# Fetching the indexer's cached keys: 128 pages a gather, through DRAM, in place of 128 small gathers

## The chip, the cores and the metric

One core of a Trainium2 chip runs the whole kernel. Its engines work side by side, each through its own list of instructions in order: TensorE (PE) multiplies matrices, VectorE (DVE) and ScalarE (ACT) do elementwise work, GpSimd (POOL) does elementwise work and issues indirect DMAs, SyncE (SP) issues the other DMAs. The metric is the device time of one launch in microseconds. One launch was also taken by the hardware profiler; its records are the profile and the trace.

## The reference

The kernel computes one layer of a hybrid decoder for a prompt of 1024 tokens and a sample group of 8 sequences with 8 new tokens each (1088 tokens, model width 1024). The layer has a sparse attention branch and a gated linear attention branch (GLA), a gated merge, an output projection and an MLP. The sparse branch selects 256 keys for each query by a small indexer:

```python
def indexer_scores(q_idx, w_idx, k_idx):
    dots = jnp.einsum('bqhd,bsd->bqhs', q_idx, k_idx) * (IDX_DIM ** -0.5)
    return jnp.einsum('bqhs,bqh->bqs', jax.nn.relu(dots), w)   # w: scaled w_idx

# sample group: 4096 past keys of each sequence lie in pages of 128 keys
k_idx_past = cache_kidx[page_table].reshape(b, past, IDX_DIM)
k_idx_all = jnp.concatenate([k_idx_past, k_idx], axis=1)
```

`cache_kidx` has 320 pages of 128 keys by 64 dimensions in float32; `page_table` names 32 pages for each of the 8 sequences, so 256 pages of 32 KB, 8 MB in all, are fetched through an index. The prompt's scores use no cache. All sums are kept to float32 quality: each operand is split into a high part, rounded to the format that TensorE multiplies at full rate, and a low part (value minus high part), and three products are added.

## The kernel before, in words

All of the first phase is written by one function, `front`. Its pieces are Python generators ("streams"): `main` runs the projections in the order of the list `jobs` (a small `misc` block with the indexer keys, four blocks `qi` of indexer queries, `ka`, `va`, four `qa`, then for each of four heads `qb`, `kb` and the GLA values `psv`, then gates); `idx_prompt` makes the prompt's scores (`psi`); `idx_sample` makes the sample group's scores; `top_prompt` searches on DVE for the prompt's selection thresholds; `heads` is the GLA; others follow later. A planner (`Order.run`, `Clock`) keeps an estimate of when each engine and each tile would be ready and steps the first stream that could go on; what it writes down is a fixed order for each engine. Every operation is issued by one helper (L219 in the profile), so groups are told apart by the tiles' names.

A projection block is loaded by SP (`wr`, 512 KB), rounded by ACT (`wh`), and its low part `wl` = `wr` - `wh` is made by GpSimd or DVE: the function `sub` chooses by the planner's clocks, with a handicap for DVE as last argument. PE then runs groups of three matmuls, for instance `qa<-xh,wh`, `qa<-xl,wh`, `qa<-xh,wl`.

`idx_sample` goes through the past keys in 16 chunks of 16 pages. `i_load(n)` fetches a chunk into a page `kir` of 128 partitions (two pages by 64 dimensions) by 1024: eight indirect DMAs on GpSimd, each with 128 rows of 512 bytes; 128 in all. Three chunks are kept ahead. `split(n)` rounds the chunk on ACT (`kih`) and subtracts on DVE (`kil`, a new page). PE makes the products for each half chunk: three matmuls `pss`; ACT takes the rectified high part `rh`, DVE the low part `rl`, and three matmuls `po` sum over heads. Two chunks are fetched at the start and a third when the stream begins; the scores themselves wait for the end of `idx_prompt`.

`top_prompt` searches 32 bits. One round counts six times over score tiles (`jk<-sc`, the long instructions) and has six small steps on 128x3 numbers between them (`ga_m`, `ga_u`, `ga_f`, `gb_m`, `gb_u`, `gb_f`). It begins when `idx_prompt` ends and shares DVE with everything else. In the GLA's first head DVE prepares `gk`, for which PE's first `psas` waits.

In the second phase, `back`, there are 64 more gathers, `cvr<-vv`, of 128 rows of 2 KB for the attention values.

Of the kernel before, what the change touches and what calls it, by code (L numbers as in the profile page):

```python
# [12 lines left out]
F32 = mybir.dt.float32  # L13
F32R = mybir.dt.float32r
# [9 lines left out]
P = 128  # L24
# [23 lines left out]
NSM = 6  # L48
NSH = 6
KAHEAD = 2  # L50
VAHEAD = 1
SCRATCH = 4096
OBLEAD = 3
# [21 lines left out]
def f32(ap):  # L75
    return ap.bitcast(F32)


def view(ap, offset, dims):
    return bass.AP(tensor=ap.tensor, offset=ap.offset + offset, ap=[list(d) for d in dims])  # L80
# [254 lines left out]
def front(ph, tc, env, A, O):  # L335
# [13 lines left out]
    def page(name, dt=F32, shape=None):  # L349
        return clock.take(pgs.tile(shape or [P, T], dt, name=name, tag="pg", bufs=NPG), name, "pg", NPG)  # L350
# [9 lines left out]
    def cst(name, shape, dt=F32):  # L360
        return cs[0].tile(shape, dt, name=name, tag=name, bufs=1)
# [20 lines left out]

    ptab = page("ptab", I32, [P, 8, 32])
    sp.dma_start(ptab, view(A["page_table"], 0, [[0, P], [32, 8], [1, 32]]))
    jobs = []
    wt = {}

# [62 lines left out]
    p_q, p_b, p_64, p_32, p_n = (pf[:, i:i + 1] for i in range(5))  # L450


    ix_i = cst("ix_i", [P, 4, 32], I32)
    pm64 = cst("pm64", [P, 1])
    dve.tensor_scalar(pm64, p_n, -64.0, None, op0=OP.add)
    dve.tensor_scalar(ix_i[0:64], ptab[0:64, 0::2, :], 64.0, p_n[0:64], op0=OP.mult, op1=OP.add)
    dve.tensor_scalar(ix_i[64:128], ptab[64:128, 1::2, :], 64.0, pm64[64:128], op0=OP.mult, op1=OP.add)
    ix_k = const("ix_k", [1, 256], I32)
    dve.tensor_scalar(ix_k, ptab[0:1].rearrange("p a b -> p (a b)"), 128.0, None, op0=OP.mult)


    raw = {}
    i_order = [(qq, p) for qq in range(4) for p in range(4)]

    def i_load(n):
        qq, p = i_order[n]
        l = page(f"kir{qq}{p}", F32, [P, 1024])
        for g in range(8):
            pg = qq * 8 + g
            pool.indirect_dma_start(out=l[:, g * P:(g + 1) * P], out_offset=None, in_=A["ciT"],  # L470
                                    in_offset=bass.IndirectOffsetOnAxis(ap=ix_i[:, p, pg:pg + 1], axis=0))
        raw[n] = l


    for c, (c0, n) in enumerate(CH):
# [38 lines left out]
    brow = csg("brow", [64, 8])  # L514
    dve.tensor_scalar(brow, cb5[:64, :8], p_b[:64], None, op0=OP.is_equal)

    i_load(0)
    i_load(1)


    bcol = csg("bcol", [P, 8, 64], BF)
# [118 lines left out]
    def idx_prompt():  # L640
        yield lambda: s_wtok.done
        for grp in ((7,), (6,), (5,), (4, 2)):
            pg = page(f"sc{grp[0]}")
            o = 0
            for qt in grp:
                scp[qt] = pg[:, o:o + (qt + 1) * P]
                o += (qt + 1) * P
        scp[3] = small("sc3")
        dve.memset(f32(qz), 0.0)
        for h in range(8):  # L650
            yield lambda: h in qis
            q = qis.pop(h)
            yield [q[:, TP:T]]
            for e in range(2):
                r = ((h + e) % 2) * 64
                for b2 in range(2):
                    o = b2 * 64
                    src = q[r:r + 64, TP:T].rearrange("p (b q) -> p b q", q=8)[:, b2::2, :]
                    dve.tensor_copy(qz[o:o + 64, :, e, o + 8 * h:o + 8 * h + 8], f32(src))
            for qt in range(2, 8):  # L660
                w = (qt + 1) * P
                for k0 in range(0, w, 512):
                    n = min(512, w - k0)
                    lq = q[:, qt * P:(qt + 1) * P]
                    yield [lq]
                    ps = bank("psi")
                    pe.matmul(ps[:, :n], lq, kkh[:, k0:k0 + n], start=True, stop=False)
                    pe.matmul(ps[:, :n], lq, kkl[:, k0:k0 + n], start=False, stop=True)
                    r = small("r")
                    act.activation(r[:, :n], ps[:, :n], AF.Relu, scale=0.125)  # L670
                    sc = scp[qt][:, k0:k0 + n]
                    wc = wtok[:, qt, h:h + 1]
                    if h == 0:
                        dve.tensor_scalar(sc, r[:, :n], wc, None, op0=OP.mult)
                    else:
                        dve.scalar_tensor_tensor(sc, r[:, :n], wc, sc, op0=OP.mult, op1=OP.add)
                if h == 7:
                    d = scp[qt][:, qt * P:w]
                    pool.affine_select(d, d, pattern=[[-1, P]], compare_op=OP.is_ge, fill=NEG, base=0, channel_multiplier=1)
# [3 lines left out]
    ss = [page("ssa", F32, [P, TP]), page("ssb")]  # L683

    def idx_sample():
        i_load(2)
        dve.memset(ss[1][0:64, TP:T], NEG)

        def split(n):
            r = raw[n]  # L690
            h = page(f"kih{n}", F32R, [P, 1024])
            l = page(f"kil{n}", F32R, [P, 1024])
            act.activation(h, r, AF.Copy)
            dve.tensor_sub(l, r, f32(h))
            raw[n] = (h, l)
        yield [raw[0]]
        split(0)
        yield lambda: s_wtok.done
        cq = iota_f("cq", [4, 8, 8], [[0, 4], [0, 8], [1, 8]])
        cb = iota_f("cb", [4, 8, 8], [[-2, 4], [1, 8], [0, 8]])  # L700
# [8 lines left out]
        wsel = cst("wsel", [P, 512], F32R).rearrange("p (e a b) -> p e a b", e=2, b=64)  # L709
        act.activation(wsel[:, 0], wsf, AF.Copy)  # L710
        dve.tensor_sub(wsel[:, 1], wsf, f32(wsel[:, 0]))
        yield lambda: s_ip.done

        def chunk(p, kh, kl, n):
# [16 lines left out]
        for qq in range(4):  # L731
            po = [bank("po0", True), bank("po1", True)]
            pend = None
            for p in range(4):
                n = qq * 4 + p
                if n + 3 < 16:
                    i_load(n + 3)
                if n + 1 < 16:
                    yield [raw[n + 1]]
                    split(n + 1)  # L740
                kh, kl = raw.pop(n)
                for e in range(2):
                    s = slice(e * 512, e * 512 + 512)
                    yield [kh[:, s], kl[:, s], qz]
                    r = chunk(p, kh[:, s], kl[:, s], 512)
                    if pend:
                        yield [pend[1][1]]
                        sums(*pend)
                    pend = (p, r, 512, po[e], p == 0, p == 3)
            yield [pend[1][1]]  # L750
            sums(*pend)
            hs = slice(qq // 2 * 64, qq // 2 * 64 + 64)
            for e in range(2):
                act.activation(ss[qq % 2][hs, e * 512:(e + 1) * 512], po[e][:64, :], AF.Copy)
                unpin(po[e])
# [842 lines left out]

    s_wtok = order.add(wtok_job(), engines=())
    s_va = []  # L1600
    s_ip = order.add(idx_prompt(), margin=M_IP)
    s_is = order.add(idx_sample(), margin=M_IS)
    s_tp = order.add(top_prompt(), engines=("dve",), slack=1.0)
# [610 lines left out]
def arrange(inp):  # L2214
    f = {k: np.asarray(v) for k, v in inp.items()}
    cont = np.ascontiguousarray
    x = np.concatenate([f["x_prompt"].reshape(TP, 1024), f["x_sample"].reshape(TS, 1024)], 0)
    w_in = f["w_in"][0]

    def fm(w, nk):  # L2220

        return cont(w.reshape(nk, P, -1, P).transpose(2, 1, 0, 3))

    c = IN_COLS
    misc = np.zeros((1024, P), np.float32)
    misc[:, 0:64] = w_in[:, c["k_i"]:c["k_i"] + 64]
    misc[:, 64:80] = w_in[:, c["a_b"]:c["a_b"] + 16]
    misc[:, 96:104] = w_in[:, c["w_i"]:c["w_i"] + 8]
    cols = [w_in[:, c["q_i"]:c["q_i"] + 512], misc, w_in[:, c["k_a"]:c["k_a"] + 256], w_in[:, :512]]
    for h in range(4):  # L2230
        cols += [w_in[:, c["q_b"] + 128 * h:c["q_b"] + 128 * (h + 1)], w_in[:, c["k_b"] + 128 * h:c["k_b"] + 128 * (h + 1)]]
    cols += [w_in[:, c["g_b"]:c["g_b"] + 1024], w_in[:, c["gate_a"]:]]
    a = {
        "xT": cont(x.T.reshape(KT, P, T)),
        "w1": fm(np.concatenate(cols, 1), 8),
        "wvb": cont(w_in[:, c["v_b"]:c["v_b"] + 1024].reshape(8, P, 4, 256).transpose(2, 1, 0, 3)),
        "wa2": cont(f["w_alpha2"][0]),
        "b_alpha": cont(f["b_alpha"][0].reshape(4, P).T),
        "gla_norm_g": cont(f["gla_norm_g"][0].reshape(2, P).T),
        "ln": cont(np.stack([f[n][0].reshape(8, P).T for n in ("ln1_g", "ln1_b", "ln2_g", "ln2_b")], 1)),  # L2240
        "wao": fm(f["w_attn_o"][0], 4),
        "wgo": fm(f["w_gla_o"][0], 8),
        "wout": fm(f["w_out"][0], 8),
        "wff1": fm(f["w_ff1"][0], 8),
        "wff2": fm(f["w_ff2"][0], 32),
        "ciT": cont(f["cache_kidx"][0].reshape(NPOOL, 32, 4, 64).transpose(0, 3, 2, 1).reshape(NPOOL * 64, P)),
        "kT": cont(f["cache_k"][0].reshape(NPOOL, 32, 4, P).transpose(0, 3, 2, 1).reshape(NPOOL * P, P)),
        "vv": cont(f["cache_v"][0].reshape(NPOOL * 32, 512)),
        "state": cont(f["state_gla"][0]),
        "page_table": cont(f["page_table"]),  # L2250
    }
    return a

# [31 lines left out]
```

## Time and profile before

| what | us |
|---|---|
| runs, median of 3 | 2206.89 (2206.7 to 2224.4) |
| profiled execution, its own time | 2213.03 |
| its span | 2211.1 |
| PE busy in the span | 2083.8 |
| DVE, ACT, POOL busy | 1359.6, 1028.3, 767.0 |
| gathers `kir<-ciT`, GpSimd busy, 128 of them | 128.8 |

Places in the span of the profiled execution: `misc` begins at 9.5, the first `qi` at 25.4, value projection `va` at 147.4, the first `psas` at 386.3. A row of a chain gives start, length and what ran; a row of waits gives who waited for whom, the total, how often and the longest; a row of windows gives a stretch and the busy time of each engine in it, PE's granted clock, the share of the DMA engines and GB/s; a row of a timeline gives start, length, engine, operation and in brackets the idle time before it with what ended it.

### The profile page before, as it was taken

How to read it: one execution, taken by the hardware profiler on the slowest of the kernel's cores; microseconds unless marked ns; L12 is line 12 of the kernel's file. 1: busy time of each engine (PE TensorE's matmuls, PEld its weight loads, DVE VectorE, ACT ScalarE, POOL GpSimd, SP SyncE). 2: the span in 40 equal slices, each digit the busy share in tenths (PEclk: the TensorE clock that was granted, in tenths of full speed). 3: DMA queues.
4: the chain of work that ended last, by engine and by line, in shares of the span. 5: the costliest groups of instructions: out<-in, count | busy, mean ns of one | idle time of the engine just before them, and what ended most of it. 6: DMA issues, size and time to landing. Idle time of an engine off the chain costs nothing.

```text
span 2211.1 us, 34794 instructions
## 1 busy us (share of the span) xinstructions
PE 2083.8 (94%) x12507; PEld 1982.6 (90%) x12507; DVE 1359.6 (61%) x2827; ACT 1028.3 (47%) x2009; POOL 767.0 (35%) x630
## 2 busy tenths in 40 slices
PE   6985998989899999999999999999999999999997
PEld 5884788879798999999999889989999999999996
DVE  4784789798825667633625864665664445457635
ACT  4652333444476666677312533444543333335443
POOL 5145632020512112122124334546455332343342
PEclk8997999999999999999999999999999999999998
DMA  5022320121212323234275314535433342135442
GB/s 174 21 81 94 119 97 29 41 68 51 78 41 93 103 77 122 75 102 162 108 260 196 140 53 123 159 120 174 127 117 119 121 141 76 65 113 174 168 152 82
DMA packets 165565, 244.02 MB, mean 110 GB/s; under 512 B 22528, under 2 KB 103424, under 8 KB 165392
## 3 DMA queue, kind: packets, MB, share of 16 engines
q1 hardware_dynamic: 156048, 216.36, 29.7%
q0 software_dynamic: 9344, 25.44, 3.8%
q8 instruction: 98, 1.61, 0.3%
q14 instruction: 75, 0.61, 0.1%
HBM read 200.61 MB, written 41.12 MB: 109 GB/s over the span
## 4 chain that ended last, share of the span: by engine, by line
PE 76%; DVE 12%; issue 4%; ACT 4%; another core or an unknown queue 2%; POOL 1%; DMA 1%; SPq 0%; DVEq 0%; ACTq 0%; POOLq 0%
PE pf L219 28%; PE gate L219 8%; PE psv L219 4%; PE pmb L219 4%; PE gb L219 3%; PE pwo L219 3%; PE psc L219 2%; PE po L219 2%; PE qi L219 2%; PE qa L219 2%; PE pma L219 2%; PE kb L219 2%; PE qb L219 2%; PE psq L219 1%
## 5 line engine op out<-in xcount | busy, mean ns | idle before, releaser
L219 PE MATMUL pf<-a,w 128*128 128x384 f32 (+1 forms) x2304 | 401.7, 330 | 3.8 <-ACT a L219 1.9
L219 PE MATMUL pf<-h,w 128*128 128x384 f32 (+1 forms) x2304 | 396.2, 329 | 2.2 <-DVE h L219 2.2
L219 PEld LDWEIGHTS pf<-a,w 128*128 128x128 f32 x2304 | 380.3, 189 | 6.4 <-ACT a L219 2.5
L219 PEld LDWEIGHTS pf<-h,w 128*128 128x128 f32 x2304 | 380.2, 189 | 4.8 <-DVE h L219 3.2
L219 POOL TENSOR_TENSOR wl<-wr,wh 128x1024 fp32r<-128x1024 f32 (+1 forms) x57 | 129.1, 2269 | 501.1 <-ACT wh L219 415.6
L219 DVE TENSOR_TENSOR w<-wr,w 128x512 fp32r<-128x512 f32 x190 | 179.4, 969 | 73.9 <-ACT w L219 73.9
L219 ACT ACTIVATE w<-wr 128x512 fp32r<-128x512 f32 x272 | 156.7, 619 | 61.7 <-PE pf L219 26.5
L219 POOL TENSOR_TENSOR a<-fr,a 128x384 fp32r<-128x384 f32 (+1 forms) x79 | 76.0, 963 | 273.9 <-ACT a L219 271.8
L219 POOL DMA_INDIRECT kir<-ciT,ix_i x128 | 128.8, 1006 | 70.2 <-issue 39.2
L219 POOL TENSOR_TENSOR w<-wr,w 128x512 fp32r<-128x512 f32 x82 | 113.1, 1391 | 80.8 <-ACT w L219 77.6
L219 PE MATMUL gate<-xh,wh 128*128 128x384 f32 (+1 forms) x384 | 131.1, 341 | 0.0
L219 PE MATMUL gate<-xl,wh 128*128 128x384 f32 (+1 forms) x384 | 126.6, 330 | 0.0
L219 PE MATMUL gate<-xh,wl 128*128 128x384 f32 (+1 forms) x384 | 126.5, 330 | 0.0
L219 DVE TENSOR_TENSOR acc<-acc,pf 128x384 f32<-128x384 f32 (+1 forms) x136 | 72.5, 537 | 87.2 <-PE pf L219 85.3
L219 ACT ACTIVATE fr<-pf 128x384 f32<-128x384 f32 (+1 forms) x96 | 45.2, 471 | 153.8 <-PE pf L219 153.1
L219 DVE TENSOR_TENSOR fr<-fr,pf 128x384 f32<-128x384 f32 (+1 forms) x96 | 50.8, 529 | 101.1 <-ACT fr L219 98.8
L219 ACT ACTIVATE wh<-wr 128x1024 fp32r<-128x1024 f32 (+1 forms) x75 | 74.2, 1005 | 67.0 <-DMA wr<-wgo 44.2
L219 DVE TENSOR_SCALAR_CACHE_REDUCE jk<-sc,gb_f 128x896 int8<-128x896 f32 (+2 forms) x96 | 92.6, 965 | 1.1
L219 ACT ACTIVATE a<-fr 128x384 fp32r<-128x384 f32 (+1 forms) x96 | 48.7, 507 | 95.1 <-DVE fr L219 93.8
L219 DVE TENSOR_SCALAR_CACHE_REDUCE jk<-sc,ga_f 128x1024 int8<-128x1024 f32 (+2 forms) x96 | 88.4, 921 | 0.9
L219 PE MATMUL psv<-wh,xh 128*128 128x256 f32 (+1 forms) x288 | 84.2, 292 | 0.0
L219 PE MATMUL psv<-wl,xh 128*128 128x256 f32 (+1 forms) x288 | 81.6, 283 | 0.0
(461 smaller groups left out, 5197.4 us busy)
## 6 DMA issues: line engine op xcount, KB each, us to landing
wr<-wff SPq DMA_DIRECT2D x256, 256.0 KB
wr<-w SPq DMA_DIRECT2D x43, 512.0 KB
ckr<-kT SPq DMA_DIRECT2D x256, 64.0 KB
ga_s<-gate SPq DMA_DIRECT2D x16, 544.0 KB
wr<-wout SPq DMA_DIRECT2D x13, 512.0 KB
mgp<-ga_s SPq DMA_DIRECT2D x16, 384.0 KB
qa_s<-qa SPq DMA_DIRECT2D x8, 544.0 KB
mgt<-ga_s SPq DMA_DIRECT2D x8, 544.0 KB
```

Source lines behind the costliest of these rows:

```text
L219: r = f(*a, **k)
```

## The change

The pages are gathered 128 at a time, an eighth of each in one gather: `ciT` is now laid out in rows of 4 KB (8 dimensions by 128 keys), a new small input `page_rows` lists the pages in the order of the chunks, and each of the 16 gathers brings 128 rows of 4 KB (512 KB) into a page `cig`. Each is then stored by SP into one of two DRAM tiles `ci_s` in page order, after which the next gather is issued; two are in flight. When the prompt's scores reach their last head (`IFROM` = 7) and all is stored, SP loads the chunks from `ci_s` (pieces of 512 bytes, 512 KB a chunk), three ahead as before. The low part is subtracted in place, in the chunk's own page, by `sub` with a handicap of 1.5 us for DVE.

```diff
+NGA = 2
+IAHEAD = 3
+IFROM = 7
+LATE_I = 1.5
...
+    ptg = cst("ptg", [P, 2], I32)
+    sp.dma_start(ptg, A["page_rows"])
...
-    ix_i = cst("ix_i", [P, 4, 32], I32)
-    pm64 = cst("pm64", [P, 1])
-    dve.tensor_scalar(pm64, p_n, -64.0, None, op0=OP.add)
-    dve.tensor_scalar(ix_i[0:64], ptab[0:64, 0::2, :], 64.0, p_n[0:64], op0=OP.mult, op1=OP.add)
-    dve.tensor_scalar(ix_i[64:128], ptab[64:128, 1::2, :], 64.0, pm64[64:128], op0=OP.mult, op1=OP.add)
+    ix_i = cst("ix_i", [P, 8, 2], I32)
+    for g in range(8):
+        dve.tensor_scalar(ix_i[:, g], ptg, 8.0, float(g), op0=OP.mult, op1=OP.add)
...
+    ci_s = [env["dram"].tile([P, 8192], F32, name=f"ci_s{i}") for i in range(2)]
+    pieces = [(i, g) for i in range(2) for g in range(8)]
+    got = deque()
+    def gather():
+        i, g = pieces.pop(0)
+        l = page(f"cig{i}{g}", F32, [P, 1024])
+        pool.indirect_dma_start(out=l, out_offset=None, in_=A["ciT"],
+                                in_offset=bass.IndirectOffsetOnAxis(ap=ix_i[:, g, i:i + 1], axis=0))
+        got.append((l, i, g))
+    def pages_in_order():
+        while got:
+            yield [got[0][0]]
+            l, i, g = got.popleft()
+            sp.dma_start(ci_s[i][:, g * 1024:(g + 1) * 1024], l)
+            if pieces:
+                gather()
...
     def i_load(n):
         qq, p = i_order[n]
-        l = page(f"kir{qq}{p}", F32, [P, 1024])
-        for g in range(8):
-            pg = qq * 8 + g
-            pool.indirect_dma_start(out=l[:, g * P:(g + 1) * P], out_offset=None, in_=A["ciT"],
-                                    in_offset=bass.IndirectOffsetOnAxis(ap=ix_i[:, p, pg:pg + 1], axis=0))
-        raw[n] = l
+        raw[n] = l = page(f"kir{qq}{p}", F32R, [P, 1024])
+        sp.dma_start(f32(l.rearrange("p (g k) -> p g k", g=8)),
+                     view(ci_s[p // 2], (p % 2 * 64 + qq * 16) * 8192, [[P, P], [16384, 8], [1, P]]))
...
-    i_load(0)
-    i_load(1)
+    for _ in range(NGA):
+        gather()
...
+            if h == IFROM:
+                flags.add("scores")
...
     def idx_sample():
-        i_load(2)
...
-            l = page(f"kil{n}", F32R, [P, 1024])
-            act.activation(h, r, AF.Copy)
-            dve.tensor_sub(l, r, f32(h))
-            raw[n] = (h, l)
-        yield [raw[0]]
-        split(0)
+            act.activation(h, f32(r), AF.Copy)
+            sub(r, f32(r), f32(h), LATE_I)
+            raw[n] = (h, r)
...
+        yield lambda: s_pg.done and "scores" in flags
+        yield ci_s
+        for n in range(IAHEAD):
+            i_load(n)
+        yield [f32(raw[0])]
+        split(0)
         yield lambda: s_ip.done
...
+    s_pg = order.add(pages_in_order(), engines=())
```

The planner then writes another order. The work on PE is the same in number; on DVE the 16 subtracts `kil` become two in place and `wl` goes from 18 to 7; on GpSimd 14 chunk subtracts are new, gathers go from 128 to 16 and `wl` from 49 to 60; on SP there are 16 stores and 16 loads more, and one load of `ptg`.

On GpSimd at the start, before (`kir` is a chunk's page, `IOTA` makes constants, `wl` is a weight's low part; each of the first three rows is eight gathers):

```order
L219 DMA kir_248<-ciT,ix_i 128x128 x8
L219 DMA kir_257<-ciT,ix_i 128x128 x8
L219 DMA kir_375<-ciT,ix_i 128x128 x8
L219 IOTA cq 128x256
L219 IOTA cb 128x256
L219 TENSOR_TENSOR wl_0_525<-wr_0_393,wh_0_524 128x1024
```

And now, at the same place:

```order
L223 DMA cig_256<-ciT,ix_i 128x1024
L223 DMA cig_258<-ciT,ix_i 128x1024
L223 TENSOR_TENSOR wl_0_281<-wr_0_140,wh_0_280 128x1024
L223 DMA cig_334<-ciT,ix_i 128x1024
L223 DMA cig_355<-ciT,ix_i 128x1024
L223 IOTA cq 128x256
L223 IOTA cb 128x256
L223 DMA cig_459<-ciT,ix_i 128x1024
L223 DMA cig_468<-ciT,ix_i 128x1024
L223 IOTA cb_476 128x512
L223 DMA cig_489<-ciT,ix_i 128x1024
L223 DMA cig_509<-ciT,ix_i 128x1024
```

The train of 24 gathers ahead of the first `wl` on GpSimd is now single gathers between casts and constants; eight more follow after one more `wl`.

On PE in the query projections `qa`, before (`pss` and `po` are the scores' two products):

```order
L219 MATMUL pss<-kih_1847,qz 128x512
L219 MATMUL pss<-kil_1848,qz 128x512
L219 MATMUL pss<-kih_1847,qz 128x512
L219 MATMUL qa_1_1982<-xh_114,wh_0_1713 128x384
L219 MATMUL qa_1_1982<-xl_122,wh_0_1713 128x384
L219 MATMUL qa_1_1982<-xh_114,wl_0_1714 128x384
L219 MATMUL qa_1_1982<-xh_115,wh_0_1713 128x384
L219 MATMUL qa_1_1982<-xl_123,wh_0_1713 128x384
L219 MATMUL qa_1_1982<-xh_115,wl_0_1714 128x384
L219 MATMUL po_1797<-rh,wsel 64x512
```

And now:

```order
L223 MATMUL pss<-kih_1762,qz 128x512
L223 MATMUL pss<-kir_1672,qz 128x512
L223 MATMUL pss<-kih_1762,qz 128x512
L223 MATMUL qa_0_1777<-xh_120,wh_0_1537 128x384
L223 MATMUL qa_0_1777<-xl_128,wh_0_1537 128x384
L223 MATMUL qa_0_1777<-xh_120,wl_0_1538 128x384
L223 MATMUL qa_0_1777<-xh_121,wh_0_1537 128x384
L223 MATMUL qa_0_1777<-xl_129,wh_0_1537 128x384
L223 MATMUL qa_0_1777<-xh_121,wl_0_1538 128x384
L223 MATMUL po_1722<-rh,wsel 64x512
L223 MATMUL po_1722<-rl,wsel 64x512
L223 MATMUL po_1722<-rh,wsel 64x512
```

Behind the `po` rows follows at once the next chunk's `pss` (of `kih_1836`). Before, some 36 to 60 matmuls of the projections stood between one chunk and the next, and the last chunk lay among the first head's `psv`; now about 12 stand there, and all 16 chunks lie between `va` and the middle of the third `qa` block.

On DVE around the last small score step `rl` (128x64), before:

```order
L219 SCALAR_TENSOR_TENSOR rl<-pss,rh 128x64
L219 TENSOR_SCALAR jk,ga_n<-sc_433,ga_f 128x640
L219 COPY_PREDICATED gb_u<-gb_m,gb_f 128x3
L219 TENSOR_SCALAR jk,ga_n<-sc_433,ga_f 128x384
L219 TENSOR_SCALAR gb_f<-gb_u 128x3
L219 TENSOR_TENSOR t_3082<-po_2975,bdm 64x64
L219 TENSOR_SCALAR t_3084<-bdm 64x64
L219 TENSOR_TENSOR ssb<-t_3082,t_3084 64x64
```

And now:

```order
L223 SCALAR_TENSOR_TENSOR rl<-pss,rh 128x64
L223 TENSOR_SCALAR jk,gb_n<-sc_411,gb_f 128x768
L223 COPY_PREDICATED ga_u<-ga_m,ga_f 128x3
L223 TENSOR_TENSOR t_2391<-po_2299,bdm 64x64
L223 TENSOR_SCALAR t_2393<-bdm 64x64
L223 TENSOR_TENSOR ssb<-t_2391,t_2393 64x64
L223 TENSOR_SCALAR jk,gb_n<-sc_413,gb_f 128x512
L223 TENSOR_SCALAR ga_f<-ga_u 128x3
L223 TENSOR_TENSOR qa_2322<-qa_0_2324,qa_2322 64x384
```

From this last `rl` to `gk`, on which the first `psas` waits, DVE's order had 4.2 rounds of the search before and has 13.2 now (six `jk` rows make a round), with twelve query subtracts like the last row among them. From the search's start to `gk` there were 16.3 rounds and are 16.8.

More of the change, by code (lines that the diff above doesn't have):

```diff
@@ L735, in idx_sample @@
                 n = qq * 4 + p
-                if n + 3 < 16:
-                    i_load(n + 3)
+                if n + IAHEAD < 16:
+                    i_load(n + IAHEAD)
                 if n + 1 < 16:
-                    yield [raw[n + 1]]
+                    yield [f32(raw[n + 1])]
                     split(n + 1)
@@ L2245, in arrange @@
         "wff2": fm(f["w_ff2"][0], 32),
-        "ciT": cont(f["cache_kidx"][0].reshape(NPOOL, 32, 4, 64).transpose(0, 3, 2, 1).reshape(NPOOL * 64, P)),
+        "ciT": cont(f["cache_kidx"][0].reshape(NPOOL, 32, 4, 64).transpose(0, 3, 2, 1).reshape(NPOOL * 8, 1024)),
         "kT": cont(f["cache_k"][0].reshape(NPOOL, 32, 4, P).transpose(0, 3, 2, 1).reshape(NPOOL * P, P)),
@@ L2250, in arrange @@
         "page_table": cont(f["page_table"]),
+        "page_rows": cont(f["page_table"].reshape(2, 2, 2, 32).transpose(1, 3, 2, 0).reshape(P, 2)),
     }
```

## The prediction

> **What bounds the kernel now.** First the page: its span, the slices and the chain.
>
> ```profile
> span 2211.1 us, 34794 instructions
> PE   6985998989899999999999999999999999999997
> PE 76%; DVE 12%; issue 4%; ACT 4%; another core or an unknown queue 2%; POOL 1%; DMA 1%; SPq 0%; DVEq 0%; ACTq 0%; POOLq 0%
> ```
>
> TensorE is full from about the eighth slice on; what is to be won lies in the first seven, about 390 us. The stretches are cut where the kernel's phases meet: second weight block, prompt indexer, then value projection to the first `psas`, then the rest.
>
> ```profile
> core 0: us, PE busy (x) PEld busy (x) DVE busy (x) ACT busy (x) POOL busy (x), PEclk, DMA share, GB/s
> 0.00:26.40 26.40, 15.45 (x78) 14.85 (x78) 18.41 (x47) 16.20 (x33) 14.65 (x23) 1.00 0.73 254
> 26.40:48.00 21.60, 10.84 (x45) 8.90 (x44) 5.19 (x8) 4.06 (x9) 15.42 (x17) 0.73 0.43 135
> 48.00:147.20 99.20, 93.98 (x504) 87.28 (x504) 83.17 (x164) 63.28 (x129) 20.07 (x16) 0.95 0.06 19
> 147.20:386.40 239.20, 195.64 (x1083) 174.68 (x1082) 176.72 (x397) 78.06 (x129) 112.76 (x106) 0.89 0.28 94
> ```
>
> PE is idle for 10.8 us of the second stretch (21.60 - 10.84) and 43.6 us of the fourth, at low clocks (0.73, 0.89). The chain of waits over the first 420 us names the loss, and the timelines of POOL and ACT show what runs beside it (start, length, operation, idle before it).
>
> ```profile
> by line: another core or an unknown queue 10.9%; PE qi L219 10.3%; PE qa L219 10.0%; PE psv L219 7.9%; issue 6.2%; PE po L219 6.1%; DVE jk L219 5.4%; DVE sc L219 5.4%; PE pss L219 3.9%; PE misc L219 3.2%; PE kb L219 2.8%; PE psi L219 2.7%;
> 163.53 23.49 another core or an unknown queue
> 13.28 1.22 POOL L219 DMA_INDIRECT kir<-ciT,ix_i  x1 [0.19 <-issue]
> 43.99 0.94 POOL L219 DMA_INDIRECT kir<-ciT,ix_i  x1 [0.30 <-issue]
> ...
> 141.51 0.98 POOL L219 DMA_INDIRECT kir<-ciT,ix_i  x1 [0.16 <-issue]
> 182.36 0.94 POOL L219 DMA_INDIRECT kir<-ciT,ix_i  x1 [0.30 <-issue]
> 187.74 0.96 POOL L219 DMA_INDIRECT kir<-ciT,ix_i  x1 [4.44 <-issue]
> 207.37 0.94 POOL L219 DMA_INDIRECT kir<-ciT,ix_i  x1 [0.30 <-issue]
> 187.05 0.44 ACT L219 ACTIVATE vf<-va 128x320 f32<-128x320 f32 x1 [23.51 <-remote]
> 210.56 1.08 ACT L219 ACTIVATE rh<-pss 128x512 fp32r<-128x512 f32 x2 [11.58 <-remote]
> ```
>
> The waits that the profile can put to no one are 10.9% of 420, 45.8 us. The one shown and its like at 199 end 3 to 4 us after a long train of gathers (141.5 to 183.3, 187.7 to 208.3): TensorE's results reach ACT only when GpSimd has stopped issuing. Issue gaps of PE in the second stretch lie in the train of 13.3 to 44.9. The other gathers of this kernel, 64 in pairs, lie where PE runs on:
>
> ```profile
> L219 POOL DMA_INDIRECT cvr<-vv,ix_v x64 | 66.4, 1038 | 19.6 <-issue 10.8 <-DMA ckr<-kT 4.2 <-DVE ckl L219 1.4
> 1327.00:1611.00 284.00, 280.25 (x1612) 262.87 (x1610) 164.75 (x310) 128.88 (x221) 143.82 (x115) 0.99 0.47 139
> ```
>
> **The change part by part.** *The extra load.* `ptg` is a second SP instruction ahead of the first weights.
>
> ```profile
> 0.82 0.39 SPq L219 DMA_DIRECT2D ptab<-page_table  x1
> ```
>
> It costs one such issue with its gap, 0.45 us, and everything behind moves by it.
>
> *Gathers, 26.4 to 48.* 24 of them become eight or so between 13 and 30 us, with casts between, and 16 in all. The loss there is 10.8 idle and (1 - 0.73) x 10.84 = 2.9 of low clock, 13.7 us. I take 12 back, keeping 1.7 for the new gathers; the ends are 5 (the shorter train still stalls) and 13.7. SP's new stores wait in its queue for each gather; behind them stand the weight loads. The next weights to be cast after the first two blocks (`wr_0_384`) stand behind two stores, and PE reaches them after some 190 more matmuls, 33 us at 0.174. 8 MB in and 8 MB out, at the 254 GB/s that the first stretch moved, take 63 us from 13 on, so until 76; the loads from DRAM wait for the last head of the prompt indexer, some 50 us later. GpSimd's later gathers wait for a page that a store has to free; behind them stands the cast of the third weight block, which PE reaches after some 300 matmuls, at 78, while 15 gathers and 8 stores (12 MB) take 47 us from 13 on, to 60. These covers gone, each microsecond of late data is one on the path. Nothing for it.
>
> *48 to 147.2.* GpSimd casts one weight more instead of DVE, PE is 95% busy: 0, between -2 and +3.
>
> *147.2 to 386.4, 239.2 us.* Here the gathers are gone, and the order packs all 16 chunks of scores into the value and first query projections, where they were spread to the end of `psv`. PE's own work is unchanged, and these pieces give its undisturbed pace:
>
> ```profile
> 224.83 6.66 PE qa L219 x42
> 305.10 3.13 PE kb L219 x18
> 321.92 7.19 PE psv L219 x60
> 308.23 1.39 PE pss L219 x6
> ```
>
> That is 0.159, 0.174, 0.120 and 0.232 us a matmul. With the counts of the order: qa 288 x 0.159 = 45.8; va, qb and kb 72 + 144 + 144 at 0.174 = 62.6; psv 222 x 0.120 = 26.6; pss 84 and po 101 at 0.232 = 42.9; transposes and gates about 3: 181 us. After the last score remain, by the order, qa 120, qb 144, kb 132 and psv 216: 19 + 25 + 23 + 26 = 93. So 88 lie in the chunk phase and 93 in the tail.
>
> The tail is DVE's. The binary search for the prompt's threshold goes on through the stretch, and DVE's order before the first `psas` now has 13.2 of its rounds after the last score, against 4.2 before, because the scores come early. A round undisturbed, and what else holds DVE:
>
> ```profile
> 321.80 1.27 DVE L219 TENSOR_SCALAR_CACHE_REDUCE jk<-sc,ga_f 128x1024 int8<-128x1024 f32 x1
> 327.89 1.28 DVE L219 TENSOR_SCALAR_CACHE_REDUCE jk<-sc,ga_f 128x1024 int8<-128x1024 f32 x1
> 343.28 0.16 DVE L219 TENSOR_SCALAR gb_m<-gb_n 128x3 int32<-128x3 f32 x1
> 353.35 2.17 DVE L219 TENSOR_SCALAR ga_m<-ga_n 128x3 int32<-128x3 f32 x1
> 372.06 1.99 DVE L219 COPY_PREDICATED gb_u<-gb_m,gb_f 128x3 int32<-128x3 int32 x1
> 377.51 1.39 DVE L219 TENSOR_SCALAR ga_m<-ga_n 128x3 int32<-128x3 f32 x1
> 384.98 1.21 DVE gk L219
> 353.13 2.36 POOL L219 TENSOR_TENSOR wl<-wr,wh 128x1024 fp32r<-128x1024 f32 x1 [44.64 <-ACT wh L219]
> PE psas L219 <- DVE gk L219: 8.0, 1, 8.0
> L219 DVE TENSOR_TENSOR kil<-kir,kih 128x1024 fp32r<-128x1024 f32 x13 | 15.8, 1218 | 0.8 <-ACT kih L219 0.7
> L219 DVE TENSOR_TENSOR qa<-qa,qa 64x384 fp32r<-64x384 f32 (+1 forms) x24 | 12.8, 533 | 11.6 <-ACT qa L219 10.1 <-issue 0.9
> ```
>
> A round is 327.89 - 321.80 = 6.09 us, so 80.4. A small step that takes 0.16 alone takes 2.17, 1.99 or 1.39 while GpSimd subtracts: on average 1.69 lost for each GpSimd operation, more than the 1.22 of a subtract (`kil`) that DVE hands over. By the order 11 stand in the tail (nine `wl`, `gq`, `gqz`): 18.6. Gate work on DVE: from the last `rl` at about 344 to `gk` at 385 are 41 us, less 4.2 rounds and five such waits (8.5), 6.9. Twelve query subtracts at 0.53: 6.4. Together 112 us against PE's 93: PE waits 19 at `psas`, where it waited 8.0. The Trainium skill, "SBUF — State Buffer", section "Who interferes with whom", says that GpSimd and a VectorE operation that needs the shared port pair block each other for a whole instruction, whoever came first; the rows agree for small steps (2.17 beside 2.36), and by that rule the hand-over speaks against this change: it costs the tail up to 11 x 2.36 = 26.
>
> The chunk phase has its own rows: `rl`, `kih`, and how long DVE and PE stood at a chunk's next step until now.
>
> ```profile
> 141.23 1.29 DVE rl L219 x2
> 283.34 1.05 ACT kih L219
> DVE rl L219 <- ACT rh L219: 27.5, 18, 8.7
> PE po L219 <- ACT rh L219: 14.9, 5, 7.5
> ```
>
> DVE has 32 `rl`, 3.7 rounds, two subtracts, 12 query subtracts and up to 17 waits for GpSimd (14 chunks, three `wl`) there: 20.6 + 22.5 + 2.4 + 6.4 + 28.7 = 81 of 88 us. It is nearly full, so PE will stand now and then; also the chunk loads are queued on SP behind `kaT` and `ka_s` stores, which wait for ACT. I take 1 us a chunk, 16, near the 14.9 of PE's row; the ends are 3 and 40. The stretch is 88 + 16 + 112 = 216, 23 less than 239.2.
>
> *Behind 386.4* the order on PE is the same and few casts change engine: 0, from -2 to +3.
>
> **Sum:** 0.45 - 12 - 23 = -34.6 against the profiled execution's 2213.0: 2178.4. The median of the runs shown is 6.1 lower, 2206.9, so 2172.
>
> **The rivals.** *A, the stall goes with bytes or has another cause.* All of the 59 us (45.8 + 13.7) then falls in 13 to 80: 0.45 - 23 + 45.8 = +23, 2230. For: the 4 KB rows bring the same bytes. Against: 0 to 26.4 moved most (254 GB/s) at clock 1.00, and the 2 KB rows of `cvr` do nothing. The Trainium skill, same page and section, has it that DMA never contends with a compute engine and that PE and ACT wait on no one, by which the gathers would be innocent; the rows above, 23.51 and 11.58 us that end with a train, do not agree.
>
> *B, the packed chunk phase.* The chain of one chunk (load, `kih`, subtract on GpSimd, `pss`, `rh`, `rl`, `po`) shows through: 1.05 + 2.36 + 0.54 + 0.65 + one DVE wait 1.69 = 6.3 instead of 1 a chunk, 85 us, so +50 and 2257. It turns slower than now by 1% from (34.6 + 22)/16 + 1 = 4.5 us a chunk on. For: rows of 27.5 and 14.9. Against: loads run three chunks ahead.
>
> *C, small gains.* Early gain 5, 30 us of waits in the chunk phase, the tail 7 longer, 11 x (2.36 - 1.69): 0.45 - 5 - 23 + 14 + 7 = -6.6, 2200.
>
> *D, more.* DVE's small steps fall beside GpSimd's work less often, and the stretch is PE's 181 and 16: 0.45 - 12 - 42 = -54, 2153.
>
> **How the numbers follow.** Forecast 0.50 (2160 to 2186), A 0.11, B 0.09, C 0.20, D 0.10. Changes of 1%, 22 us, are what a measurement of this kernel tells from none. Faster: 0.47 + 0.10 + a quarter of C = 0.62; slower: B and half of A = 0.15; 0.23 between. The range 2146 to 2212 holds forecast, C and D.
>
> **What would show it.** Right: no wait on "another core" or "remote" over 4 us before `psas`; PEclk near 1 in 26 to 48; PE's wait for `gk` about 19; the first `psas` near 352. Wrong: gaps of PE beside the new gathers before 80 us (A); PE waiting for `rl` or `kir` over 60 us in all (B); a DVE tail under 95 or over 120 us.

## The result

The changed kernel took 2149.8 us (median of four runs, 2148.8 to 2150.9) against 2211.7 (2206.7 to 2224.4): a ratio of 0.971, interval 0.967 to 0.976. The forecast of 2172 had the direction and a little over half of the size. A later section shows that this ratio belongs to some chips and not to others; which chip these first runs met isn't on record.

The page of the changed kernel, the rows that answer to those of before:

```profile
span 2149.2 us, 34662 instructions
PE   7999988998999999998999999999999999999997
PE 69%; DVE 17%; issue 5%; ACT 4%; DMA 2%; POOL 2%; SPq 0%; DVEq 0%; ACTq 0%; POOLq 0%
```

"Another core or an unknown queue" is gone from the chain, and DVE has risen from 12% to 17%. To see where 61.9 us of span went, both traces are cut at the same places in the program: first `qi`, a further 22.6 us, first `ka`, first `va`, last score (`po`), first `psas`. Before:

```profile
25.40:48.00 22.60, 11.84 (x51) 9.80 (x50) 6.14 (x10) 4.06 (x9) 16.11 (x18) 0.74 0.41 129
48.00:119.60 71.60, 69.04 (x371) 65.21 (x371) 56.76 (x117) 41.28 (x86) 8.29 (x4) 0.94 0.05 16
119.60:147.30 27.70, 25.05 (x136) 22.13 (x135) 26.52 (x49) 22.09 (x43) 11.88 (x12) 1.00 0.08 26
147.30:345.30 198.00, 162.42 (x872) 142.91 (x871) 135.95 (x313) 61.60 (x104) 99.58 (x100) 0.88 0.32 106
345.30:386.30 41.00, 33.04 (x210) 31.61 (x210) 40.57 (x85) 16.36 (x25) 13.09 (x6) 0.94 0.11 37
```

And after (stretch, its length, busy PE, PEld, DVE, ACT, POOL, clock, DMA share, GB/s):

```profile
25.10:47.70 22.60, 21.02 (x125) 19.54 (x124) 17.56 (x36) 11.78 (x26) 14.89 (x14) 1.00 0.87 321
47.70:103.60 55.90, 53.92 (x296) 50.21 (x296) 49.63 (x100) 34.34 (x71) 10.13 (x8) 0.97 0.47 188
103.60:123.40 19.80, 19.80 (x114) 18.75 (x113) 18.18 (x35) 16.04 (x33) 5.99 (x6) 1.00 0.22 60
123.40:219.80 96.40, 90.51 (x468) 75.14 (x467) 72.79 (x133) 53.75 (x90) 43.56 (x20) 0.98 0.55 164
219.80:329.50 109.70, 93.27 (x618) 91.78 (x618) 108.17 (x262) 30.20 (x49) 22.58 (x10) 0.94 0.22 76
```

| stretch | before | after | difference | forecast |
|---|---|---|---|---|
| to the first `qi` | 25.4 | 25.1 | -0.3 | +0.45 |
| first `qi` to first `va` | 121.9 | 98.3 | -23.6 | -12 |
| first `va` to last score | 198.0 | 96.4 | -101.6 | |
| last score to first `psas` | 41.0 | 109.7 | +68.7 | |
| (the two together) | 239.0 | 206.1 | -32.9 | -23 |
| behind the first `psas` | 1824.8 | 1819.7 | -5.1 | 0 |

The early stretch and the chunk phase lose little now. In the first 22.6 us of the queries PE does 125 matmuls where it did 51, at clock 1.00 instead of 0.74, though the DMAs move 321 GB/s instead of 129. The tail is longer by 68.7 us, most of it PE's own work: 618 matmuls (93.27 us) lie behind the last score now, 210 (33.04 us) did before. The search has more of its rounds there too, and PE's wait for `gk` at the end of the tail has doubled from 8.0 us. The waits of PE (sum, count, longest):

```profile
PE psas L223 <- DVE gk L223: 26.0, 3, 16.4
PE po L223 <- DVE rl L223: 5.6, 3, 5.1
```

The first row has three waits, 16.4 the longest, that of the first head. The second row belongs to the chunk phase.

### The profile page after: what moved, and what is told of

It is laid out like the page before. It is cut to its first block, busy times and chain, and to the rows that moved or that the text cites. A ratio compares the mean times of both kernels' runs of the same rounds, so it can differ in the third digit from the quotient of the medians.

```text
span 2149.2 us, 34662 instructions
## 1 busy us (share of the span) xinstructions
PE 2061.4 (96%) x12492; PEld 1965.4 (91%) x12507; DVE 1347.3 (63%) x2806; ACT 1030.8 (48%) x2010; POOL 717.0 (33%) x543
## 4 chain that ended last, share of the span: by engine, by line
PE 69%; DVE 17%; issue 5%; ACT 4%; DMA 2%; POOL 2%; SPq 0%; DVEq 0%; ACTq 0%; POOLq 0%
PE pf L223 30%; PE gate L223 8%; DVE jk L223 5%; PE pwo L223 3%; PE psc L223 2%; PE psv L223 2%; PE po L223 2%; PE pmb L223 2%; PE gb L223 2%; PE qi L223 1%; PE pob L223 1%; PE psq L223 1%; PE pov L223 1%; PE ppt L223 1%; PE psi L223 1%
## 5 line engine op out<-in xcount | busy, mean ns | idle before, releaser
L223 POOL TENSOR_TENSOR wl<-wr,wh 128x1024 fp32r<-128x1024 f32 (+1 forms) x68 | 156.1, 2300 | 546.4 <-ACT wh L223 450.3
L223 ACT ACTIVATE w<-wr 128x512 fp32r<-128x512 f32 x272 | 156.8, 619 | 49.1 <-PE pf L223 26.4
L223 PE MATMUL psv<-wh,xl 128*128 128x256 f32 (+1 forms) x288 | 81.3, 282 | 0.0
```

Of the source, the lines that this page charges most:

```text
L223: r = f(*a, **k)
```

## The experiments

Two theories stood at the start. Mine: trains of short-row gathers (many gathers issued one behind the other) hold up PE, and their removal is the gain. The rival: the gathers are innocent and the new order, the low parts in place among it, makes the gain.

**Spare gathers in the changed kernel.** Where GpSimd is idle and PE full, 14 gathers were put behind each of two weight casts, into room that nobody reads.

```diff
         sub(l, r, f32(h), ...)
         e[0], e[1] = h, l
+        if i in (4, 5):
+            for j in range(14):
+                pool.raw.indirect_dma_start(out=spare[:128, j % 4], out_offset=None, in_=A["kT"],
+                    in_offset=bass.IndirectOffsetOnAxis(ap=ix_i[:128, j % 8, 0:1], axis=0))
...
+    spare = csg("spare", [P, 4, P])
```

> The changed kernel with 28 spare gathers added on GpSimd, 14 behind each of two weight casts of the query-indexer blocks (about 68.8 to 86 and 88.6 to 106 us), each 128 rows of 512 bytes of the key cache into spare room that nobody reads. There GpSimd stands idle and PE is busy for 20.00 of 20 us in the changed kernel. My theory (a train of short-row gathers holds up PE's traffic with the others until the train ends): PE loses 5 to 12 us in each train, so about 2160 to 2174 us against 2150, with waits named remote or unknown queue that end with the trains. Rival (the gathers are innocent, the stalls of before came from something else): PE stays full there and the time stays at 2149 to 2152 us.

Measured, in one run on chip 0: 2145.3 us, and PE never stopped beside the spare gathers. The first spare train in its timeline (start, duration of the first and the last gather):

```profile
65.07 0.97 POOL L414 DMA_INDIRECT spare<-kT,ix_i  x1
84.23 1.10 POOL L414 DMA_INDIRECT spare<-kT,ix_i  x1 [0.30 <-issue]
```

and the windows over it and over the second spare train, which ends at 107, from the same kernel:

```profile
66.00:88.00 22.00, 22.00 (x126) 20.77 (x125) 20.88 (x38) 14.66 (x30) 17.86 (x16) 1.00 0.47 175
88.00:108.00 20.00, 20.00 (x115) 18.95 (x114) 19.26 (x38) 14.20 (x29) 16.02 (x15) 1.00 0.17 47
```

My theory, 2160 to 2174 us, missed on this chip. The same with 16 rows a gather:

> The same 28 spare gathers at the same places, but of 16 rows each. If the stall goes by the number of gather instructions or by GpSimd's time in them, the loss is that of the kernel with 128 rows (10 to 24 us). If it goes by rows (one descriptor set for each), an eighth of it, under 3 us, so 2149 to 2153 us.

It took 2146.5 us in one run on chip 0, PE full again. With nothing lost to the 128 rows either, it tells nothing of rows or instructions.

**The order of before without gathers.** Each chunk comes by one SP load of 512 KB from a fixed run of pages; the planner was still told of the gathers, so the order stays. The kernel leaves out the page table for these loads, so it scores other keys; PE's matmuls are the same in number.

```diff
+        sp.raw.dma_start(l.rearrange("p (g k) -> p g k", g=8),
+                         view(A["ciT"], n * 1024 * P, [[P, P], [P * P, 8], [1, P]]))
         for g in range(8):
-            pg = qq * 8 + g
-            pool.indirect_dma_start(out=l[:, g * P:(g + 1) * P], out_offset=None, in_=A["ciT"],
-                                    in_offset=bass.IndirectOffsetOnAxis(ap=ix_i[:, p, pg:pg + 1], axis=0))
+            clock.note("pool", "indirect_dma_start", (), dict(out=l[:, g * P:(g + 1) * P], in_=A["ciT"]))
```

> The kernel before, with its order kept on every engine, but each chunk is loaded by one SP DMA of 512 KB in pieces of 512 bytes from a fixed run of 16 pages instead of eight gathers on GpSimd; it leaves out the page table for the scores. My theory (the gather trains cause both the early loss and that of the score chunks): from the first qi to va 122 falls to 98 to 103, from va to the last po 198 falls to 150 to 160 (PE's own work there is 148), the tail stays at 41, so 2211 - 20 - 43 = 2140 to 2156 us, as fast as the changed kernel. Rival (the packed order and the low parts in place give the gain): it stays at 2190 to 2212 us.

Measured: 2138.8 us. The same cuts (first `qi`, first `va`, last score, first `psas`):

```profile
26.20:129.60 103.40, 98.00 (x553) 90.86 (x553) 87.19 (x173) 66.99 (x138) 15.60 (x11) 1.00 0.17 50
129.60:274.80 145.20, 145.20 (x872) 133.33 (x871) 135.36 (x312) 62.57 (x103) 0.00 (x0) 1.00 0.43 135
274.80:315.90 41.10, 33.12 (x213) 31.71 (x211) 40.67 (x85) 16.35 (x25) 13.08 (x6) 0.94 0.12 37
```

These are about the stretches that I expected, a little shorter in the middle (145.2 for 150 to 160): in the old order PE has not one idle moment in the chunk phase, and the tail is the 41 us of before. But on chip 0, where the first four experiments ran, the kernel before itself took 2146.7 to 2156.5 us in 13 runs, median 2150.7, not 2211. Against them the ratio is 0.993 (0.992 to 0.995), and the gain of some 60 us that my theory drew from the trace was not there to be had. The time is about my 2140 to 2156, but not for my reason. This run shows that the old order, with direct loads, is no slower than the new one (the changed kernel, on other chips, took 2144.7 to 2149.8); it does not show what the old order without gathers takes on a chip that stalls, and no run does.

**Low parts on DVE alone.**

```diff
-            sub(r, f32(r), f32(h), LATE_I)
+            dve.tensor_sub(r, f32(r), f32(h))
```

> The changed kernel with all 16 low parts subtracted on DVE, none on GpSimd. By my terms DVE takes 14 x 1.22 more and is spared 14 waits of 1.69, 6.6 less in the chunk phase, which PE bounds now (90.5 of 96.4 us): the same within 4 us, 2146 to 2154. Rival (handing the low parts to GpSimd is what pays): 14 x 1.22 = 17 us slower, 2160 to 2170.

Measured on chip 0: 2152.1 us, 1.001 of the kernel before there (1.000 to 1.002). That is inside my 2146 to 2154. The changed kernel itself did not run on that chip; on chip 9, where the kernel before is as fast, it took 2144.7, so the share that goes to GpSimd may be worth some 7 us. If so, not in the chunk phase alone: the first `psas` came at 323.7 with DVE alone and at 326.4 in the changed kernel on chip 9. The chunk phase was 3.8 us longer and the tail 5.6 shorter; what was lost lies behind the first `psas`, 4.1 us before the gates and 3.1 in them. My terms had spared DVE 6.6 us in the chunk phase. Neither 0 nor 17 fits that well, and two chips are compared: it stays open.

**The two kernels again, on chip 7.**

> The kernel before, as it is, with a profile on the chip of these runs, since runs of it beside the first four experiments took 2146.7 to 2156.5 us where it took 2206.7 to 2224.4 earlier. Theory S (the stall beside gather trains comes with the chip or the moment, not with the kernel): 2147 to 2157 us, its 128 gathers issued as before at 0.95 us each, no wait of ACT named remote, PE full from 26 to 48 and from 147 to 300 us. Theory G (the gather trains always stall PE): 2205 to 2225 us, waits of 23 and 11 us as before.

> The changed kernel on the same chip beside it. Theory S: 2145 to 2152 us, so about the same as the kernel before there (ratio 0.995 to 1.003): what the new order gains in the chunk phase it gives back at psas. Theory G: 0.97 as measured first.

On chip 7 the kernel before took 2209.0 (its other 13 runs 2214.1), the changed one 2148.7: a ratio of 0.971 (0.968 to 0.973). Its trace of the kernel before has the stalls again, at slightly other places. Among the waits of its first 400 us ("remote" is a releaser that the profile can't name):

```profile
ACT rh L219 <- remote: 31.5, 4, 12.7
ACT vf L219 <- remote: 13.3, 2, 7.1
ACT wtok L219 <- remote: 10.6, 1, 10.6
```

and in the window of the first 22 us of the queries, where PE does 44 matmuls:

```profile
26.40:48.00 21.60, 11.25 (x44) 9.38 (x44) 5.02 (x8) 4.28 (x9) 15.34 (x17) 0.73 0.42 135
```

So theory S holds against G by the times: the same program takes 2150 on one chip and 2210 on another. Each chip that the record names was met once, so a cause in the chip and one in the moment are not told apart; "chip" below means both. No trace of the kernel before was taken on a chip where it takes 2150, so that its own trains pass there without a stall follows from the times alone. What S left open is whether a train is what stalls.

**Spare gathers in the kernel before.** The edit is that of the first experiment, in the kernel before, the second train with 16 rows.

> The kernel before, its order and its own 128 gathers kept, with 28 spare gathers of 512-byte rows added where GpSimd is idle and PE full: 14 of 128 rows each from about 72 us on, and 14 of 16 rows each from about 101 us on. Two chips have told of two kernels before: 2147 to 2157 us on one, 2205 to 2217 on the other. Theory S (the stall beside a gather train is there on some chips only): where the kernel before takes about 2210, PE and ACT stall in the train of 72 to 90 us too, 5 to 12 us, so 2215 to 2225; where it takes about 2150, no train stalls anything, not those of 13 to 45 and 141 to 236 us either, and the time stays within 4 us. Rival (the stall needs the kernel's own data, not a train): where it takes 2210, the spare train costs nothing. Rows or instructions: if the cost goes by rows, the train of 16 rows stalls nothing on either chip.

This ran once on chip 11, where the one run of the kernel before took 2207.9. Here the spare train does stall PE. Its first and last gather in the timeline:

```profile
73.35 0.98 POOL L409 DMA_INDIRECT spare<-kT,ix_i  x1 [0.16 <-issue]
91.30 0.94 POOL L409 DMA_INDIRECT spare<-kT,ix_i  x1 [0.30 <-issue]
```

and the windows along it, of the same kernel:

```profile
72.00:80.00 8.00, 8.00 (x44) 7.29 (x44) 7.84 (x20) 5.85 (x15) 6.47 (x6) 1.00 0.40 105
80.00:86.00 6.00, 5.91 (x30) 4.75 (x28) 4.57 (x11) 3.06 (x7) 4.63 (x5) 1.00 0.15 45
86.00:91.00 5.00, 2.44 (x11) 1.68 (x10) 2.80 (x6) 0.89 (x3) 4.08 (x4) 1.00 0.20 52
91.00:100.00 9.00, 8.15 (x43) 7.02 (x44) 7.58 (x16) 6.42 (x16) 0.94 (x1) 1.00 0.06 16
```

Without the spare train, the kernel before on chip 7 in the same 5 us:

```profile
86.00:91.00 5.00, 5.00 (x29) 4.61 (x28) 4.94 (x11) 4.02 (x9) 0.00 (x0) 1.00 0.02 3
```

For 12 us of the train PE runs on, then it does 11 matmuls in 5 us instead of 29, and as the train ends it recovers. These gathers carry 64 KB each, nobody reads what they bring, and the kernel's own data play no part: on such a chip a train of 14 is enough. PE stands idle for 2.6 us, then 0.9, which is less than the 5 to 12 us of theory S. The time was 2213.0, 5 us above the one run of before; single runs show nothing here, since the 13 runs of the kernel before on chip 7 spread over 11 us. On chip 0 a train of the same kind cost nothing. The train of 16 rows shows no gap named issue on PE, but DVE's work holds PE there (PE 10.73 busy of 14 us), so rows against instructions stays open.

**Breaking the trains.**

```diff
                                     in_offset=bass.IndirectOffsetOnAxis(ap=ix_i[:, p, pg:pg + 1], axis=0))
+            if g % 4 == 3:
+                for j in range(4):
+                    pool.raw.memset(spare, 0.0)
...
+    spare = csg("spare", [P, 512])
```

> The kernel before with its order kept, where GpSimd clears a spare tile four times (0.525 us each, 2.1 us in all) after every four gathers, so that no unbroken train is longer than 5 us; it leaves out nothing. In the kernel with the spare train the stall began some 12 us into it and ended with it, and trains of 8 stall nothing. Theory L (a stall needs an unbroken train of 10 us or more): on a chip where the kernel before takes about 2210, the stalls go and 2150 to 2170 us are left, with chunks up to 4 us later. Theory N (each gather adds to the stall, pauses or not): 2205 to 2225. On a chip where the kernel before takes about 2150, within 6 us of it, and its trace shows what trains do there.

It met chip 9, where the kernel before took 2149.3, so L and N could not be told apart, and it was not within 6 us: 2216.1, a ratio of 1.031 (1.028 to 1.034). In the first 22 us of the queries PE is full, and no wait in the first 400 us is named remote:

```profile
26.40:48.00 21.60, 21.60 (x134) 21.14 (x133) 6.05 (x10) 3.85 (x8) 18.19 (x24) 1.00 0.40 124
```

The chain of waits over the first 400 us, by line, says what took the time:

```profile
by line: POOL kir L219 28.6%; POOL spare L475 14.3%; issue 13.6%; DVE sc L219 7.7%; DVE jk L219 5.8%; PE psv L219 5.2%; DVE qi L219 2.0%; DMA kir<-ciT,ix_i 1.8%; PE po L219 1.7%; DVE cu L219 1.6%; DVE qz L219 1.6%; DMA xr<-xT 1.6%; POOL sc 
```

GpSimd itself is the bound there: the pauses have 14.3% of the 400 us, 57 us, on the path, and the kernel became 67 us slower. I take from it that, where nothing stalls, the old gathers are just about paced by GpSimd's 1.25 us an instruction (0.95 and a gap of 0.30), so that a delay of it lands on the path; without a trace of the kernel before on such a chip this is inferred.

> The changed kernel on the chip of these runs. Where the kernel before takes about 2210: 0.97 of it. Where it takes about 2150: 2143 to 2150, a ratio of 0.996 to 1.000, since the gathers then cost little to remove.

The changed kernel took 2144.7 us on the same chip, 0.9975 of the kernel before (0.9965 to 0.9985): as expected. The same program, 40 to 60 us, over its train of eight gathers, on chip 7:

```profile
40.00:60.00 20.00, 17.61 (x86) 15.72 (x85) 15.39 (x37) 11.16 (x24) 10.18 (x9) 0.91 1.03 410
```

and on chip 9:

```profile
40.00:60.00 20.00, 19.41 (x109) 17.90 (x108) 17.74 (x40) 12.92 (x27) 10.31 (x9) 1.00 1.02 397
```

On chip 7 there are 86 matmuls, on chip 9 109. Even the new gathers seem to cost something where the old ones stalled: the first `va` comes at 123.3 there and at 119.9 on chip 9, which is most of the 4 us between 2148.7 and 2144.7.

**The wait for `gk`.** Two edits of the changed kernel test how I priced its tail. The search pauses after 13 rounds until the first head's `gk` is written:

```diff
         for i in range(31, -1, -1):
+            if i == 18:
+                yield lambda: "gk" in flags
...
         yield from gla_pre(h)
+        flags.add("gk")
```

> The changed kernel, where the prompt's search pauses after 13 of its 32 rounds until gk of the first head is written. If the tail is DVE's, as I priced it (13.2 rounds of 6.09 after the last score), four rounds fewer stand ahead of gk, 24 us of DVE against PE's wait of 16.4 us at psas: the wait goes, 10 to 16 us faster than the changed kernel. Rival (the rounds come back later on the path, ahead of the attention that needs the search): no faster than by 3 us.

And the nine weight casts ahead of `gk` go to DVE at the same places (`move` for weight blocks 10 to 16):

```diff
+            if move:
+                dve.raw.tensor_sub(out, a, b)
+                clock.note("pool", "tensor_tensor", (out, a, b), dict(op=OP.subtract))
+                return
...
-            sub(l, r, f32(h), WLATE if 1 < state["job"] < mix_at - 1 else 0.0)
+            sub(l, r, f32(h), WLATE if 1 < state["job"] < mix_at - 1 else 0.0, 10 <= i <= 16)
```

> The changed kernel with its order kept, but the nine low parts of weights that GpSimd makes between the last score and gk are made by DVE at the same places. If each GpSimd subtract costs DVE 1.69 us of waiting, DVE gains 15.2 and pays 9 x 1.22 = 11.0: gk 4 us earlier, PE's wait at psas 12 instead of 16. Rival (the waits are smaller than I priced them): gk up to 11 us later.

On chip 7, beside the changed kernel's 2148.7 (2146.5 to 2150.7), the first took 2144.7 (2141.7 to 2145.1), the second 2146.9 (2143.8 to 2148.7), a difference that four runs each do not tell from none. With the pause, PE's wait for `gk` (sum, count, longest):

```profile
PE psas L223 <- DVE gk L223: 15.4, 4, 8.8
```

and the window from the last score to the first `psas`:

```profile
219.60:306.30 86.70, 86.28 (x576) 84.73 (x576) 82.12 (x193) 29.27 (x47) 18.17 (x8) 1.00 0.26 90
```

With the casts on DVE, the same wait:

```profile
PE psas L223 <- DVE gk L223: 21.7, 3, 12.1
```

and the same window:

```profile
222.90:328.80 105.90, 93.81 (x619) 92.31 (x618) 103.98 (x267) 30.21 (x49) 3.87 (x2) 0.95 0.22 77
```

The second bears out the price of a GpSimd subtract: the tail is 3.8 us shorter (109.7 to 105.9), the wait 12.1 for an expected 12. But the first `psas` is only 0.5 us earlier (328.8 for 329.3 on chip 7), since the chunk phase, in which only one of the nine casts lies, took 99.2 us for 96.4. With the pause PE is full to the first `psas` and reaches it 23 us earlier, in a changed order that has 42 of the matmuls behind it; at the first gate block 11.4 us are left, and at the end 5.9 in the profiled executions and 4 by the medians, less than the 10 to 16 that I expected and hardly more than the rival's 3. The rival had a point: 114 `jk` counts of the search now lie between `psas` and the gates where 91 lay, and PE's waits for `gk` behind the first are about 15 us for 9.6. A smaller part goes in the gates (3.1 us) and behind them (2.4 us), where PE waits 2.2 us for DVE's counts in the sample's search (`jka`).

> The changed kernel with both edits that shortened gk's way: the prompt's search pauses after 13 rounds until gk of the first head is written, and the nine low parts of weights ahead of gk are made on DVE. Alone they gave 4.0 and 1.8 us beside the changed kernel. If they add up, 5 to 7 us faster than the changed kernel; if the pause had already freed PE of the wait that the second shortens, 4 us and no more.

On chip 9: 2149.0 (2147.0 to 2149.7) against 2144.7 (2141.2 to 2147.5) of the changed kernel there, so 4 us slower, which neither line foresaw. The first `psas` comes at 306.3 as with the pause alone, 20.1 us ahead of the changed kernel on this chip (326.4), so the casts on DVE bring nothing more there. All of the 20.1 is lost again behind it, 12.6 us of it before the gates and 4.8 in them. DVE has the casts as well as the late rounds to do; that this is why was not followed. The pause alone beat the changed kernel by 0.2%, on one chip.

## Why the prediction came out as it did

The direction and the mechanism held: where the gather trains stalled PE, taking them out gave the gain. The time lies close to the lower end of the range (2146), and that it lies inside is also luck: on chips like 0 and 9 a forecast of 35 us less would have met 5. Of the signs named beforehand, no wait is called remote ahead of `psas`, the clock from 26 to 48 is 1.00 and the wait for `gk` is 16.4 for 19; the first `psas` came at 329.5, not near 352. Step by step:

*The extra load*, +0.45: the first `qi` came 0.3 us earlier. Nothing hangs on it.

*Gathers, 26.4 to 48*, -12: right. 9.2 us more PE work in the same 22.6 us, and the clock at 1.00 instead of 0.74, are 9.2 + 3.1 = 12.3.

*48 to 147.2*, 0: this step failed. The stretch to `va` gained 23.6, so another 11.3 came from here. Three things were left out. The new order does two chunks behind `va`: 23 matmuls fewer here, 5.3 us at 0.232. PE's idle time fell from 5.2 to 2.0 us, the wait of 2.7 us for the `rl` of these chunks with it. And the low clock, which I had priced up to 48 only, went on behind the stall. The kernel before:

```profile
48.00:52.00 4.00, 4.00 (x15) 4.00 (x15) 2.45 (x6) 1.33 (x4) 0.00 (x0) 0.50 0.00 0
52.00:56.00 4.00, 4.00 (x24) 4.00 (x24) 1.47 (x3) 0.92 (x3) 0.00 (x0) 0.81 0.00 0
```

In these 8 us the clock took 2.8 us ((1 - 0.50) x 4 + (1 - 0.81) x 4). By the rows of the result the clock cost 4.1 us from 48.0 to 119.6, and 1.6 in the changed kernel, 2.5 less. 5.3 + 3.2 + 2.5 are 11.0 of the 11.3. That DVE, late with its work after the stall, then held PE is not so. The order of before without gathers took 103.4 us from the first `qi` to `va`, 18.5 less, and PE waited for DVE there as long as before. From 48 to 147.3 in the kernel before, then from 26 to 130 without gathers:

```profile
PE po L219 <- DVE rl L219: 2.7, 2, 1.7
PE psi L219 <- DVE qi L219: 2.6, 2, 2.0
PE po L219 <- DVE rl L219: 2.8, 2, 1.9
PE psi L219 <- DVE qi L219: 2.6, 2, 2.0
```

Its 18.5 us are the idle time of the stall and the clock: 16.0 us idle became 5.4, and the 7.2 us of low clock became none, 17.8 together.

*Chunk phase*, 88 + 16 = 104: 96.4. PE was busy for 90.5, near the count though the 88 left out the two chunks moved here; its idle time was 5.9 instead of 16. That term was mis-sized by 10 us. Why is in part argued: the loads ran three chunks ahead, and the one row of waits is the 5.6 us for `rl` above.

*Tail*, 112 with PE waiting 19: 109.7 and 16.4. The rounds, read from the order, held: 80 `jk` counts, 13.3 rounds. So did the wait for a GpSimd subtract. The tail's 79 small steps took 27.7 us, and 14.4 with the casts on DVE; eight of the nine casts lie in the tail, so each cost 1.7. The ninth fell before it, and `gq` and `gqz` cost less than priced: the small steps lost some 14.7 us to GpSimd (27.7 - 79 x 0.165), not 18.6.

*Behind `psas`*, 0: -5.1. It lies in the gate blocks, whose window of before is

```profile
710.60:1043.80 333.20, 325.99 (x2113) 318.50 (x2113) 199.38 (x588) 232.87 (x481) 70.73 (x51) 0.99 0.34 109
```

and of after

```profile
654.40:982.90 328.50, 324.09 (x2109) 316.03 (x2109) 193.54 (x581) 229.49 (x477) 70.77 (x51) 0.99 0.35 110
```

It is there with the old order and no gathers too (gates from 640.6 on, `pmb` from 973.7: 333), so it is not the gathers' removal that gains it; which wait it is was not followed.

*The rivals.* A did not come: the changed kernel's gathers bring the same bytes at 321 GB/s without that stall, and on chip 11 a train of 64 KB gathers makes one. What was called the end of a stall 3 to 4 us behind a train is 3.8 and 2.3 us in the two rows shown, and on chip 11 a wait of ACT ended before the train did. By the rule of the Trainium skill ("SBUF — State Buffer", section "Who interferes with whom") cited with A the gathers would be innocent. The traces from chips 0 and 9 agree with it, those from chips 7 and 11 do not. B did not come, C neither. D, at 2153, was nearest in time, but by another mechanism than its own: DVE's waits in the tail stayed about as priced, and the gain lay ahead of it. What none of the cases had is that the stall depends on the chip, or on the moment it is met.

## What to carry to other kernels

A stall that the profile can name no releaser for should be looked for on another chip before an edit is credited with removing it; here one chip's trace promised 60 us where another has 5 to give. When a stall is priced, look behind its end too: the clock was still at 0.50 and 0.81 in the 8 us after it, and a window that ends with the stall misses that. And moving work early is only half a gain when a search or another filler then piles up ahead of the next thing that PE needs; the rounds in the written order told that wait to 3 us.

## What the runs showed of the hardware

The same kernel before took 2146 to 2157 us on chips 0 and 9 and 2205 to 2217 on chips 7 and 11 (a single run on 11). In the traces from 7 and 11, and in the first, PE's issue and its signals to ACT fall behind some 12 to 17 us into an unbroken train of gathers of 128 short rows; PE then moves in fits and starts, and recovers about when the train ends. In the one trace from chip 0 with such trains, two spare ones of 14, PE stays full. What differs between the chips no trace here shows. The train of eight in the changed kernel cost a few microseconds on chip 7; beside the longer ones of the kernel before, PE stood idle for some 7 to 19 us each in the first trace. After a stall the granted clock was 0.50 for 4 us and 0.81 for the next 4, with PE full.
